# First loads, zero products, an early sine and norm, and turned blocks between products, in one decoder layer

## The chip, the cores and the metric

The kernel runs on one core of a Trainium2 chip. The metric is device time of one execution in microseconds. Three runs of the kernel before gave 999.52, 999.82 and 1001.32, so the median is 999.82.

## The reference, cut to what matters

One layer works on x of 256 tokens and 2048 channels, all in float32.

```python
h = rmsnorm(x, pre_mix_norm)
z = h @ w_in                       # 2048 -> 2048 conv (GLU) | 768 q latent | 512 kv latent | 64 rotary key
a, g = split(conv_in); u = a * sigmoid(g)
u = causal_depthwise_conv(u, conv_w, conv_b)            # 31 taps, 1024 channels
u = silu(layernorm(u))
q = rmsnorm(q_lat) @ w_uq ; kv = rmsnorm(kv_lat) @ w_ukv   # 8 heads, rotary parts with cos, sin
attn = causal_attention(q, k, v)
x = x + rmsnorm(concat(rmsnorm(u), rmsnorm(attn)) @ w_out)
x = x + rmsnorm(SwiGLU(rmsnorm(x)))                        # 2048 -> 5632 -> 2048
```

The scale of the first norm (one number per token) is not applied to h: the products with `w_in` are made from x times the gain, and the scale is applied to their results. So the products can start before the norm of x is known.

## The kernel before, in words

Weights come from memory as float32. Each is split into two float16 parts: ScalarE writes the high part (`whi`, line 108) and VectorE the rest (`wlo`, line 109). A product of two such numbers is three products on TensorE: high by high (line 153), high by low (line 154) and low by high (line 155), in `mm3`. A block of 128 input channels (one k) with two blocks of 128 tokens is thus six products of 512 columns.

`Weights.load` (line 124) brings a weight in pieces. One DMA fills a tile of `stage`, of which there are four, and one split fills a tile each of `whi` and `wlo`, of which there are eight. An ordinary piece is 1 MB, four k of 512 columns. The first weight, `wg0`, comes in pieces of 1, 1, 2, 2, 2, 4 and 4 k (line 211), each in a tile of its own, and `load_x` brings the same k of the transposed x ahead of each and splits them (lines 181 to 184). A piece can be fetched only when its stage tile has been read by both splits. All these loads stand in the DMA queue of SyncE (SP), one behind the other.

The second weight, `wg1`, follows. Its third piece has the two halves of x itself ahead of it in the queue (`load_tokens`, line 214). Behind `wg1` come four small loads: the rotary frequencies, the positions, the taps and the vectors of the convolution (lines 221 to 227). From the first two, VectorE makes the angles (lines 231 to 250) and ScalarE their sines (line 251). From x itself ScalarE makes four sums of squares (line 259), from which `r_half` and `r_x` follow by VectorE and GpSimd (POOL).

Then there is a loop over four groups of 512 columns (line 303): `mm3`, then for each block of tokens a tanh (line 312), a scaled copy (line 314), a product on VectorE (line 316), two transposes on TensorE (line 319) and a copy into `upad` (line 320). Behind each group `pump` issues some taps of the convolution: 3, 8, 13 and 14 (line 36). A tap is two multiply-adds on VectorE (line 289), or two products on ScalarE (line 295) and one addition on VectorE (line 297). Taps depend on `upad` and the taps before, and fill VectorE between other work. Three groups of 448 columns follow for the latents and the rotary key (line 357), with 11, 16 and 9 taps behind them. The norms of the latents are made in `latent_norm` (line 339), whose results are transposed by DMAs in the SP queue (line 346), and the rotary key is turned, with a transpose on TensorE (lines 371 to 386). Queries, values, attention, the output product and the feed-forward part follow.

The order of instructions on each engine is drawn at compile time, by a scheduler that takes the earliest written instruction that is ready by its own estimate of times. What is written later can so be put ahead of what its estimate has as not ready. On the chip each engine keeps that order. `add_manual_dep` with `NO_SYNC` adds an order, without a wait between engines.

Of the kernel before, what the change touches and what calls it, by code (L numbers as in the profile page):

```python
# [10 lines left out]
F16 = mybir.dt.float16  # L11
# [6 lines left out]
P = 128  # L18
# [17 lines left out]
PUMPS = dict(conv=(3, 8, 13, 14), lat=(11, 16, 9), v=(1, 0), uqp=3, head=(2, 7, 4, 8, 4, 4, 9, 8))  # L36
NG = 22
# [23 lines left out]
def hymba_layer(ctx: ExitStack, tc: tile.TileContext, x, xT, pos, inv_freq, g_pre, w_in, w_lat,  # L61
# [45 lines left out]
    def split(hi, lo, src, scale):  # L107
        nc.scalar.activation(hi, src, AF.Copy, scale=scale)  # L108
        nc.vector.scalar_tensor_tensor(lo, src, scale, hi, op0=ALU.mult, op1=ALU.subtract)  # L109
# [6 lines left out]
    class Weights:  # L116
# [7 lines left out]
        def load(self, src, scale, first=None, before=None):  # L124

            n = self.n
            per = self.kpb
            k0 = 0
            pieces = list(first or [])
            while k0 < self.kt:  # L130
                kk = pieces.pop(0) if pieces else per
                kk = min(kk, self.kt - k0)
                st = stage.tile([P, 2048], F32, tag="stage", name=nm("st"))
                if before is not None:
                    before(k0, k0 + kk)
                nc.sync.dma_start(st[:, : kk * n], src[:, k0 * n : (k0 + kk) * n])
                for j in range(0, kk, self.kpb):
                    w = min(self.kpb, kk - j) * n
                    hi = wsp.tile([P, 2048], F16, tag="whi", name=nm("whi"))
                    lo = wsp.tile([P, 2048], F16, tag="wlo", name=nm("wlo"))  # L140
                    split(hi[:, :w], lo[:, :w], st[:, j * n : j * n + w], scale)
                    for i in range(min(self.kpb, kk - j)):
                        self.parts.append((hi[:, i * n : (i + 1) * n], lo[:, i * n : (i + 1) * n]))
                k0 += kk
            return self

    def mm3(ps, x_of, wgt, tbs=(0, 1), k0=0, start=True, stop=True):
# [26 lines left out]
    nc.scalar.dma_start(gpre, g_pre)  # L174
    nc.vector.tensor_scalar(gpre, gpre, X_S, None, op0=ALU.mult)
# [35 lines left out]
    wg0 = Weights(KD, 512).load(w_in[0], W_S, first=[1, 1, 2, 2, 2, 4, 4], before=load_x)  # L211
    h_of = flat(hpool_h, hpool_l)

    def load_tokens(k0, k1):
# [5 lines left out]
    ifreq = const.tile([P, HALF], F32, name="ifreq")  # L220
    nc.sync.dma_start(ifreq, inv_freq)
    pos_i = const.tile([P, NTB], I32, name="pos_i")
    nc.sync.dma_start(pos_i, pos)
    cw = region(26.5, (CB, TAPS))
    nc.sync.dma_start(cw, conv_w)
    cv = const.tile([P, 4, CB], F32, name="cv")
    nc.sync.dma_start(cv, conv_v)
# [3 lines left out]
    nc.vector.tensor_copy(pos_f, pos_i)  # L231
# [25 lines left out]
    for tb in range(NTB):  # L257
        for i in range(2):
            nc.scalar.activation(junk_tile(1024), x_sb[:, tb, i * 1024 : (i + 1) * 1024], AF.Square,
                                 accum_out=ss_x[:, 2 * tb + i : 2 * tb + i + 1])  # L260
# [42 lines left out]
    for j in range(4):  # L303
        if j == 0:
            ps = ps0
        else:
            wgt = wg1 if j == 1 else Weights(KD, 512).load(w_in[j], W_S)
            ps = [acc_tile(), acc_tile()]
            mm3(ps, h_of, wgt)
        for tb in range(NTB):  # L310
            th = work.tile([P, 256], F32, tag="A", name=nm("th"), bufs=3)
            nc.scalar.activation(th, ps[tb][:, 256:512], AF.Tanh, scale=r_half[:, tb : tb + 1])
# [4 lines left out]
            tp = tmp_tile()  # L317
            for i in range(2):
                nc.tensor.transpose(tp[:, i * P : (i + 1) * P], u[:, i * P : (i + 1) * P], ident)
            nc.scalar.copy(upad[:, 2 * j : 2 * j + 2, PAD + tb * P : PAD + (tb + 1) * P],  # L320
                           tp[:, : 2 * P].rearrange("p (c t) -> p c t", c=2))
        conv_todo += [(j, k) for k in range(TAPS)]
        pump(PUMPS["conv"][j])

# [32 lines left out]
    for j in range(3):  # L357
        wgt = Weights(KD, LN).load(w_lat[j], W_S)
        ps = [acc_tile()[:, :LN], acc_tile()[:, :LN]]
        mm3(ps, h_of, wgt)  # L360
# [627 lines left out]
```

## Time and profile before

| what | us |
|---|---|
| median of three runs | 999.82 |
| time of the profiled execution | 1001.55 |
| its span in the trace | 999.70 |
| TensorE busy in the span | 959.6 |
| VectorE busy | 876.3 |
| ScalarE busy | 578.1 |

The 1.85 us between the profiled time and its span lie around the traced work. The span is the sum of the time in which TensorE works and the time in which it waits, so a stage is read by what TensorE waits for in it, and by the clock at which it works. Most of the kernel lies behind the stages that the change touches: these end at about 180 us.

### The profile page before, as it was taken

What the parts mean: (1) busy time and instruction counts of PE and PEld (TensorE: products, weight loads), DVE (VectorE), ACT (ScalarE), POOL (GpSimd) and SP (SyncE); (2) the same over time, 40 slices, a digit from 0 to 9 for tenths busy, and PEclk for the clock granted to TensorE, in tenths of its full rate; (3) what the DMA queues carried; (4) which work ended last, traced back from release to release, by engine and by line L of the source; (5) the groups of instructions that cost most, each with busy time, mean ns of one, the idle gap of its engine ahead of it and who ended that gap; (6) DMA issues with size and microseconds to landing.
All of it is one profiled execution on the core that took longest, in us unless ns stands there. A gap on an engine that the chain in (4) does not pass through costs nothing.

```text
span 999.7 us, 11980 instructions
## 1 busy us (share of the span) xinstructions
PE 959.6 (96%) x4577; PEld 454.4 (45%) x4577; DVE 876.3 (88%) x1024; ACT 578.1 (58%) x632; POOL 33.6 (3%) x50
## 2 busy tenths in 40 slices
PE   6999997999899998999999999999999999999995
PEld 2444553775444443444444444444444444444442
DVE  6799999999967999989898997897996988899855
ACT  7796764664666555655656645654663565555521
POOL 0000000033100100000000000000000000000000
PEclk9999998999999999999999999999999999999998
DMA  8974656476654966776875874784686646645532
GB/s 340 346 262 126 243 197 192 154 247 211 211 210 118 325 167 197 256 278 197 320 214 178 317 236 155 272 288 156 220 309 234 218 185 246 238 175 220 210 127 85
DMA packets 84010, 221.95 MB, mean 222 GB/s; under 512 B 55792, under 2 KB 56432, under 8 KB 61424
## 3 DMA queue, kind: packets, MB, share of 16 engines
q1 hardware_dynamic: 83232, 220.26, 63.7%
q10 hardware_dynamic: 720, 0.93, 0.3%
q8 instruction: 36, 0.59, 0.2%
q14 instruction: 22, 0.18, 0.1%
HBM read 204.25 MB, written 4.19 MB: 209 GB/s over the span
## 4 chain that ended last, share of the span: by engine, by line
PE 60%; DVE 23%; issue 5%; ACT 4%; DMA 3%; POOL 1%; SPq 0%; DVEq 0%; POOLq 0%; ACTq 0%
PE acc L740 10%; PE acc L741 10%; PE acc L739 10%; PE tmp L741 6%; PE tmp L740 6%; PE tmp L739 6%; DVE wlo L695 6%; DVE arena L289 3%; DVE wlo L109 3%; DVE st L709 2%; PE acc L155 2%; PE acc L153 2%; PE acc L154 2%; DMA st<-in_w_gu 2%; POOL sm L207 1%
## 5 line engine op out<-in xcount | busy, mean ns | idle before, releaser
L694 ACT ACTIVATE whi<-st 128x2048 f16<-128x2048 f32 (+1 forms) x177 | 317.1, 1798 | 228.7 <-PE acc L741 77.6
L695 DVE SCALAR_TENSOR_TENSOR wlo<-st,whi 128x2048 f16<-128x2048 f32 (+1 forms) x177 | 375.2, 2150 | 52.9 <-ACT whi L694 52.5
L740 PE MATMUL acc<-wlo,arena 128*128 128x512 f16 x620 | 235.0, 379 | 4.7 <-DVE wlo L695 4.7
L739 PE MATMUL acc<-whi,arena 128*128 128x512 f16 x620 | 235.0, 379 | 2.5 <-DVE q L773 1.4
L741 PE MATMUL acc<-whi,arena 128*128 128x512 f16 x620 | 235.0, 379 | 0.0
L153 PE MATMUL acc<-whi,arena 128*128 128x512 f16 (+1 forms) x380 | 143.5, 378 | 5.5 <-ACT whi L108 5.5
L741 PEld LDWEIGHTS <-arena 128*128 128x128 f16 x951 | 93.0, 98 | 117.4 <-issue 5.6
L154 PE MATMUL acc<-wlo,arena 128*128 128x512 f16 (+1 forms) x380 | 143.4, 377 | 2.2 <-DVE wlo L109 2.0
L740 PEld LDWEIGHTS <-arena 128*128 128x128 f16 x951 | 93.0, 98 | 114.3 <-issue 2.4
L739 PEld LDWEIGHTS <-arena 128*128 128x128 f16 x951 | 93.0, 98 | 113.3 <-DVE a L796 1.2
L155 PE MATMUL acc<-whi,arena 128*128 128x512 f16 (+1 forms) x380 | 143.3, 378 | 0.0
L739 PE MATMUL tmp<-whi,arena 128*128 128x512 f16 x331 | 125.4, 379 | 0.0
L740 PE MATMUL tmp<-wlo,arena 128*128 128x512 f16 x331 | 125.4, 379 | 0.0
L741 PE MATMUL tmp<-whi,arena 128*128 128x512 f16 x331 | 125.4, 379 | 0.0
L109 DVE SCALAR_TENSOR_TENSOR wlo<-st,whi 128x2048 f16<-128x2048 f32 (+4 forms) x59 | 118.2, 2009 | 6.5 <-ACT whi L108 6.5
L709 DVE TENSOR_TENSOR st<-st 128x1024 f32<-128x1024 f32 x135 | 117.2, 868 | 4.1
L108 ACT ACTIVATE whi<-st 128x2048 f16<-128x2048 f32 (+4 forms) x59 | 98.5, 1677 | 34.4 <-PE acc L155 10.3
L289 DVE SCALAR_TENSOR_TENSOR arena<-arena 128x256 f32<-128x256 f32 x184 | 78.5, 488 | 0.0
L153 PEld LDWEIGHTS <-arena 128*128 128x128 f16 x380 | 37.8, 99 | 47.4 <-ACT arena L113 5.0
L155 PEld LDWEIGHTS <-arena 128*128 128x128 f16 x380 | 37.8, 99 | 44.8 <-issue 5.1
L154 PEld LDWEIGHTS <-arena 128*128 128x128 f16 x380 | 37.6, 99 | 42.3 <-issue 2.8
L295 ACT ACTIVATE x_sb<-arena 128x256 f32<-128x256 f32 x56 | 25.3, 506 | 10.1 <-DVE arena L297 10.1
(209 smaller groups left out, 667.9 us busy)
## 6 DMA issues: line engine op xcount, KB each, us to landing
st<-in_w_gu SPq DMA_DIRECT2D x88, 1024.0 KB, 5.5
st<-in_w_dn SPq DMA_DIRECT2D x44, 1024.0 KB, 5.0
st<-in_w_out SPq DMA_DIRECT2D x16, 1024.0 KB, 5.1
st<-in_w_in SPq DMA_DIRECT2D x14, 1024.0 KB, 9.2
st<-in_w_lat SPq DMA_DIRECT2D x12, 896.0 KB, 5.5
x_sb<-in_x SPq DMA_DIRECT2D x4, 1024.0 KB, 8.6
st<-in_w_uqn SPq DMA_DIRECT2D x4, 768.0 KB, 4.9
st<-in_w_uv SPq DMA_DIRECT2D x2, 1024.0 KB, 5.9
```

Source lines behind the costliest of these rows:

```text
L108: nc.scalar.activation(hi, src, AF.Copy, scale=scale)
L109: nc.vector.scalar_tensor_tensor(lo, src, scale, hi, op0=ALU.mult, op1=ALU.subtract)
L153: nc.tensor.matmul(p_ap, xh, wh, start=(start and k == 0), stop=False)
L154: nc.tensor.matmul(p_ap, xh, wl, start=False, stop=False)
L155: nc.tensor.matmul(p_ap, xl, wh, start=False, stop=(stop and k == wgt.kt - 1))
L289: nc.vector.scalar_tensor_tensor(cacc[:, cb, :], upad[:, cb, k : k + S], cw[:, cb, k : k + 1], cacc[:, cb, :], op0=ALU.mult, op1=ALU.add)
L694: self.chain("ACT", nc.scalar.activation(hi[:, :n], src, AF.Copy, scale=scale))
L695: self.chain("DVE", nc.vector.scalar_tensor_tensor(lo[:, :n], src, scale, hi[:, :n], op0=ALU.mult, op1=ALU.subtract))
L709: self.chain("DVE", nc.vector.tensor_tensor(d, p, m, op=ALU.add))
L739: nc.tensor.matmul(ps, ah, bh, start=key not in self.begun, stop=False)
L740: nc.tensor.matmul(ps, ah, bl, start=False, stop=False)
L741: nc.tensor.matmul(ps, al, bh, start=False, stop=last)
```

## The change

- The pieces of `wg0` keep their sizes, but pieces 1, 1, 2 share one tile of `stage`, `whi` and `wlo`, and so do pieces 2, 2. The whole weight takes four tiles of each kind.
- A tile of zeros is set by VectorE, one sine of one column of it is made on ScalarE, and seven products of 512 columns of these zeros stand first on TensorE. Their result is not read.
- Frequencies and positions are loaded from ScalarE's queue at the start. The two halves of x, the taps and the vectors are loaded ahead of the second piece of `wg1` rather than the third.
- Three orders are added: the cast of the positions stands behind the last split of `wg0` on VectorE, the squares of the second half of x behind the first high part of `wg1` on ScalarE, and the first tanh behind its second high part.
- The work behind a group is parted in two. `glu` makes tanh, copy and product at once. `turn` holds the transposes, the copy into `upad` and the taps, and is called inside the next group's `mm3`: ahead of its k = 6 in group 1, of its k = 3 in groups 2 and 3 and in the first latent group. So it is also written behind the load of the next weight and no longer ahead of it.

The short description of the change also names a rotary key ahead of taps and sums over channel blocks by pairs. The diff, whose core follows, has no line on either.

```diff
+WARM = 7
+    def behind(ins, other):
+        tc.add_manual_dep(ins.ins, other.ins.name, NO_SYNC, reason="order")
...
-        def load(self, src, scale, first=None, before=None):
+        def load(self, src, scale, pieces=(), before=None):
+            for k0 in range(0, self.kt, self.kpb):
+                kb = min(self.kpb, self.kt - k0)
                 st = stage.tile([P, 2048], F32, tag="stage", name=nm("st"))
+                hi = wsp.tile([P, 2048], F16, tag="whi", name=nm("whi"))
+                lo = wsp.tile([P, 2048], F16, tag="wlo", name=nm("wlo"))
+                j = 0
+                while j < kb:
+                    kk = pieces.pop(0) if pieces else kb
+                    c = slice(j * n, (j + kk) * n)
+                    if before is not None:
+                        before(k0 + j, k0 + j + kk)
+                    nc.sync.dma_start(st[:, c], src[:, (k0 + j) * n : (k0 + j + kk) * n])
+                    h, self.last = split(hi[:, c], lo[:, c], st[:, c], scale)
+                    self.his.append(h)
+                    j += kk
...
+    def mm3(ps, x_of, wgt, tbs=(0, 1), k0=0, start=True, stop=True, at=()):
         for k in range(wgt.kt):
+            if k in at:
+                at[k]()
...
+    zeros = region(20, (512,), F16)
+    nc.vector.memset(zeros, 0.0)
+    nc.scalar.activation(zeros[:, 0:1], zeros[:, 0:1], AF.Sin)
+    warm = tmp_tile()
+    for i in range(WARM):
+        nc.tensor.matmul(warm, zeros[:, 0:P], zeros, start=True, stop=True)
+    ifreq = const.tile([P, HALF], F32, name="ifreq")
+    nc.scalar.dma_start(ifreq, inv_freq)
+    pos_i = const.tile([P, NTB], I32, name="pos_i")
+    nc.scalar.dma_start(pos_i, pos)
...
-    wg0 = Weights(KD, 512).load(w_in[0], W_S, first=[1, 1, 2, 2, 2, 4, 4], before=load_x)
+    wg0 = Weights(KD, 512).load(w_in[0], W_S, pieces=(1, 1, 2, 2, 2), before=load_x)
...
-        if k0 == 8:
+        if k0 == 4:
             for tb in range(NTB):
                 nc.sync.dma_start(x_sb[:, tb, :], x[:, tb, :])
+            nc.sync.dma_start(cw, conv_w)
+            nc.sync.dma_start(cv, conv_v)
...
-    nc.vector.tensor_copy(pos_f, pos_i)
+    behind(nc.vector.tensor_copy(pos_f, pos_i), wg0.last)
...
+            if tb == 1:
+                behind(sq, wg1.his[0])
...
+    def glu(j, ps):
+        us = []
         for tb in range(NTB):
...
+            if j == 0:
+                behind(t, wg1.his[1])
...
+            us.append(u)
+        def turn():
+            for tb, u in enumerate(us):
+                tp = tmp_tile()
+                for i in range(2):
+                    nc.tensor.transpose(tp[:, i * P : (i + 1) * P], u[:, i * P : (i + 1) * P], ident)
+                nc.scalar.copy(upad[:, 2 * j : 2 * j + 2, PAD + tb * P : PAD + (tb + 1) * P],
+                               tp[:, : 2 * P].rearrange("p (c t) -> p c t", c=2))
+            conv_todo.extend((j, k) for k in range(TAPS))
+            pump(PUMPS["conv"][j])
+        return turn
+    turn = glu(0, ps0)
+    for j in range(1, 4):
+        wgt = wg1 if j == 1 else Weights(KD, 512).load(w_in[j], W_S)
+        ps = [acc_tile(), acc_tile()]
+        mm3(ps, h_of, wgt, at={6 if j == 1 else 3: turn})
+        turn = glu(j, ps)
...
-        mm3(ps, h_of, wgt)
+        mm3(ps, h_of, wgt, at={3: turn} if j == 0 else ())
```

## Rows read from the trace of the kernel before

**Rows 1.** The page, busy time of each engine (share of the span) and instructions.

```profile
PE 959.6 (96%) x4577; PEld 454.4 (45%) x4577; DVE 876.3 (88%) x1024; ACT 578.1 (58%) x632; POOL 33.6 (3%) x50
```

**Rows 2.** Waits from 0 to 300: total us, times, longest us.

```profile
PE tmp L385 <- DVE kp L384: 6.2, 1, 6.2
...
PE tmp L319 <- DVE u L316: 2.4, 3, 1.0
```

**Rows 3.** Windows of 20 us: length, busy by engine, clock, DMA.

```profile
40.00:60.00 20.00, 19.47 (x94) 9.17 (x93) 18.50 (x39) 18.03 (x27) 0.00 (x0) 1.00 0.69 242
...
100.00:120.00 20.00, 20.00 (x108) 10.45 (x108) 20.00 (x31) 13.27 (x15) 0.00 (x0) 1.00 0.87 303
```

**Rows 4.** Timeline of TensorE, start: start, length, instruction, idle before and releaser.

```profile
5.51 0.59 PE L153 MATMUL acc<-whi,arena 128*128 128x512 f16 x1 [5.51 <-ACT whi L108]
...
10.88 0.63 PE L153 MATMUL acc<-whi,arena 128*128 128x512 f16 x1
12.12 0.38 PE L154 MATMUL acc<-wlo,arena 128*128 128x512 f16 x1 [0.61 <-DVE wlo L109]
12.34 0.38 PE L155 MATMUL acc<-whi,arena 128*128 128x512 f16 x1
...
21.68 0.38 PE L154 MATMUL acc<-wlo,arena 128*128 128x512 f16 x1 [1.41 <-DVE wlo L109]
```

**Rows 5.** Timeline of ScalarE, 0 to 56 us.

```profile
3.13 1.28 ACT L113 ACT_TABLE_LOAD   x1 [3.13 <-DMA arena<-in_xT]
4.43 0.51 ACT L113 ACTIVATE arena<-arena,gpre 128x256 f16<-128x256 f32 x1
...
17.39 1.91 ACT L108 ACTIVATE whi<-st 128x2048 f16<-128x2048 f32 x1 [0.78 <-DMA st<-in_w_in]
...
26.19 1.91 ACT L108 ACTIVATE whi<-st 128x2048 f16<-128x2048 f32 x1 [0.65 <-DMA st<-in_w_in]
...
31.78 1.06 ACT L259 ACTIVATE junk<-x_sb 128x1024 bf16<-128x1024 f32 x1 [0.84 <-DMA x_sb<-in_x]
...
35.73 0.47 ACT L312 ACTIVATE th<-acc,r_half 128x256 f32<-128x256 f32 x1 [1.62 <-DVE row_u L594]
...
44.58 1.28 ACT L251 ACT_TABLE_LOAD   x1
...
53.18 1.28 ACT L312 ACT_TABLE_LOAD   x1
```

**Rows 6.** Timeline of VectorE: a split, the cast of the positions, the first taps.

```profile
19.33 2.29 DVE L109 SCALAR_TENSOR_TENSOR wlo<-st,whi 128x2048 f16<-128x2048 f32 x1 [1.80 <-ACT whi L108]
...
40.25 0.16 DVE L231 CAST pos_f<-pos_i 128x2 f32<-128x2 int32 x1
...
48.31 2.46 DVE L289 SCALAR_TENSOR_TENSOR arena<-arena 128x256 f32<-128x256 f32 x6
```

**Rows 7.** Timeline of the SP queue: two late issues of first pieces.

```profile
6.21 0.35 SPq L136 DMA_DIRECT2D st<-in_w_in  x1
...
12.10 4.21 SPq L136 DMA_DIRECT2D st<-in_w_in  x3
```

**Rows 8.** Windows of 1 us, columns as in Rows 3: DMA early and full.

```profile
5.00:6.00 1.00, 0.49 (x1) 0.19 (x2) 0.96 (x2) 0.85 (x2) 0.00 (x0) 1.00 0.62 160
...
14.00:15.00 1.00, 1.00 (x7) 0.47 (x5) 1.00 (x3) 0.79 (x2) 0.00 (x0) 1.00 1.01 426
```

**Rows 9.** Timeline of ScalarE at the end of the latent groups.

```profile
154.35 1.06 ACT L108 ACTIVATE whi<-st 128x1024 f16<-128x1024 f32 x1 [3.96 <-DMA st<-in_w_uk]
157.28 1.48 ACT L108 ACTIVATE whi<-st 128x1536 f16<-128x1536 f32 x1 [1.88 <-DMA st<-in_w_uqn]
158.67 0.62 ACT L362 ACTIVATE arena<-acc,r_x 128x448 f32<-128x448 f32 x1
```

**Rows 10.** Timeline of TensorE there.

```profile
162.63 0.48 PE L385 MATMUL tmp<-ident,kp 128*128 128x128 f32 x1 [6.24 <-DVE kp L384]
...
168.62 0.38 PE L153 MATMUL acc<-whi,arena 128*128 128x512 f16 x1
```

More of the change, by code (lines that the diff above doesn't have):

```diff
@@ L107, in split @@
     def split(hi, lo, src, scale):
-        nc.scalar.activation(hi, src, AF.Copy, scale=scale)
-        nc.vector.scalar_tensor_tensor(lo, src, scale, hi, op0=ALU.mult, op1=ALU.subtract)
+        h = nc.scalar.activation(hi, src, AF.Copy, scale=scale)
+        return h, nc.vector.scalar_tensor_tensor(lo, src, scale, hi, op0=ALU.mult, op1=ALU.subtract)
+    def behind(ins, other):
+        tc.add_manual_dep(ins.ins, other.ins.name, NO_SYNC, reason="order")
     def split_g(hi, lo, src, g):
@@ L122, in __init__ @@
             self.parts = []
-        def load(self, src, scale, first=None, before=None):
+        def load(self, src, scale, pieces=(), before=None):
             n = self.n
[L127 to L132, printed above, removed]
-                st = stage.tile([P, 2048], F32, tag="stage", name=nm("st"))
[L134 to L144, printed above, removed]
+            pieces = list(pieces)
+            self.his = []
+            for k0 in range(0, self.kt, self.kpb):
+                kb = min(self.kpb, self.kt - k0)
+                st = stage.tile([P, 2048], F32, tag="stage", name=nm("st"))
+                hi = wsp.tile([P, 2048], F16, tag="whi", name=nm("whi"))
[10 more added lines that the diff above has]
+                    j += kk
+                for i in range(kb):
+                    self.parts.append((hi[:, i * n : (i + 1) * n], lo[:, i * n : (i + 1) * n]))
@@ L145, in load @@
             return self
-    def mm3(ps, x_of, wgt, tbs=(0, 1), k0=0, start=True, stop=True):
+    def mm3(ps, x_of, wgt, tbs=(0, 1), k0=0, start=True, stop=True, at=()):
         for k in range(wgt.kt):
+            if k in at:
+                at[k]()
             wh, wl = wgt.parts[k]
@@ L208, in rstd_of @@
         return r
-    wg0 = Weights(KD, 512).load(w_in[0], W_S, first=[1, 1, 2, 2, 2, 4, 4], before=load_x)
+    wg0 = Weights(KD, 512).load(w_in[0], W_S, pieces=(1, 1, 2, 2, 2), before=load_x)
     h_of = flat(hpool_h, hpool_l)
+    cw = region(26.5, (CB, TAPS))
+    cv = const.tile([P, 4, CB], F32, name="cv")
     def load_tokens(k0, k1):
-        if k0 == 8:
+        if k0 == 4:
             for tb in range(NTB):
                 nc.sync.dma_start(x_sb[:, tb, :], x[:, tb, :])
+            nc.sync.dma_start(cw, conv_w)
+            nc.sync.dma_start(cv, conv_v)
     wg1 = Weights(KD, 512).load(w_in[1], W_S, before=load_tokens)
[L220 to L227, printed above, removed]
     ps0 = [acc_tile(), acc_tile()]
@@ L258, in hymba_layer @@
         for i in range(2):
-            nc.scalar.activation(junk_tile(1024), x_sb[:, tb, i * 1024 : (i + 1) * 1024], AF.Square,
-                                 accum_out=ss_x[:, 2 * tb + i : 2 * tb + i + 1])
+            sq = nc.scalar.activation(junk_tile(1024), x_sb[:, tb, i * 1024 : (i + 1) * 1024], AF.Square,
+                                      accum_out=ss_x[:, 2 * tb + i : 2 * tb + i + 1])
+            if tb == 1:
+                behind(sq, wg1.his[0])
     ss_t = smalls(2)
@@ L301, in pump @@
             conv_tap(*conv_todo.pop(0))
[L303 to L308, printed above, removed]
-            mm3(ps, h_of, wgt)
+    def glu(j, ps):
+        us = []
         for tb in range(NTB):
             th = work.tile([P, 256], F32, tag="A", name=nm("th"), bufs=3)
-            nc.scalar.activation(th, ps[tb][:, 256:512], AF.Tanh, scale=r_half[:, tb : tb + 1])
+            t = nc.scalar.activation(th, ps[tb][:, 256:512], AF.Tanh, scale=r_half[:, tb : tb + 1])
+            if j == 0:
+                behind(t, wg1.his[1])
             av = work.tile([P, 256], F32, tag="B", name=nm("av"), bufs=3)
@@ L316, in hymba_layer @@
             nc.vector.scalar_tensor_tensor(u, th, 1.0, av, op0=ALU.add, op1=ALU.mult)
[L317 to L323, printed above, removed]
+            us.append(u)
[15 more added lines that the diff above has]
+        turn = glu(j, ps)
     z_all = region(16, (NTB, KL + QL + ROPE))
```

1 line of the change is left out of this document (removed).

## The prediction

> **What bounds the kernel now.** I read the page first: TensorE is busy for 959.6 of 999.7 us [rows 1], so it waits for only 40 us, and a change saves what it takes from these waits or from the time at half clock. Then I asked the view of waits for the stages that the diff touches: up to 300 us TensorE has one wait of 6.2 us before the transpose of the rotary key, three before the transposes of the conv groups, 2.4 us together [rows 2], and two for low parts of the first weight, 0.61 and 1.41 us [rows 4]. The windows say why so little else: TensorE works all the time and VectorE nearly does, 18.50 us of 20 from 40 to 60 and 20.00 from 100 to 120, yet between 22 and 153 us no product waits for a split [rows 2, 3]. TensorE is the bound there, and VectorE is full because taps fill it. So whatever brings TensorE forward before 153 us goes through, as long as splits stay ahead.
>
> The timelines of the start give the order there. TensorE waits 5.51 us for its first product, works at half clock for 13 products (0.63 us each, 5.37 us from the first to the thirteenth, so 0.45 us apart) and at full clock from 12.12 on (0.38 us each, the next start 0.215 behind, 512 columns at 2.4 GHz and a little) [rows 4]. At 21.68 it has waited 1.41 us for the low part of the sixth piece (k = 8 to 11). That low part is made from 19.33 to 21.62 [rows 6], behind a high part of 17.39 to 19.30 that waited for its DMA [rows 5]. So the path to 21.68 is landing, 1.91 us on ScalarE, 2.29 us on VectorE. From there TensorE does not wait before 55 us.
>
> **Part 1, pieces that share tiles.** Seven pieces in seven stage tiles, of which there are four, make SP wait: the fifth piece is issued at 6.21 and the last at 12.10 [rows 7]. Meanwhile the DMA engines are not full: 160 GB/s from 5 to 6 us, where the full rate is 426 [rows 8]. With four tiles for the whole weight nothing is waited for, and the queue is full from its first byte to the end of `wg0`. What that is worth: the gap lies between 4 and 7 us. If the small pieces run at about 340 GB/s at best, some 0.15 MB are won in each of these three us, 0.45 MB in all, 1.1 us at 426 GB/s. If they could run at 426, it is 0.27 MB each, 0.8 MB, 1.9 us, and a little more behind 7 us. The lower bound is 0, should the small loads that now run beside them cost as much as is won. I take 1.4 us, near the first, since small pieces are what runs there: the sixth piece lands at 16.0, its low part is ready at 20.2, and the products behind it run 1.4 us earlier.
>
> TensorE must by then be through with k = 0 to 7. These are 48 products: from about 5.8 us on, with all 13 slow ones kept, 13 x 0.45 + 35 x 0.215 = 13.4 us, the end at 19.2. That is before 20.2, so this part holds without any help from the zero products.
>
> **Part 2, zero products and the sine first.** The zeros are ready when VectorE has set them, the table for the sine is loaded (1.28 us, as at 44.58) and one column is done, an estimate of 2.7 us. Seven products 0.45 us apart last to 5.8, about where the first real one starts now. The table load of 3.13 no longer stands between the first x and its split [rows 5]: ScalarE starts 1.3 us earlier, less up to 0.4 us for issuing two small loads. So the first real product is ready earlier but waits for the zeros: nothing won or lost there, between -0.5 and 0.5 us. What the zeros could give is full clock earlier: at most 13 x (0.45 - 0.215) = 3.0 us of slow products. I take 0 of it for the sum, because the low part at 20.2 ends last either way. It would pay only if landing gained more than 2.4 us.
>
> The clock needs work, and it lasts over the wait of 1.41 us: the product at 21.68 takes 0.38 us, as before it [rows 4]. After 6.24 us without products it is down [rows 10]. The Trainium skill (TensorE: Matmul & The Clock Gate, Part 1: The HAM clock gate) has it that slow is the default and sustained activity releases it, with the moment set by a window that runs freely. By that rule the zeros buy full clock some 3 us sooner, and since the moment varies this also makes the start vary; the sum by it is the same, by the paragraph above.
>
> For the table, Sin is now followed by copies without a load, as behind 44.58, and the next load stands before the first tanh. One of three loads goes (3.13, 44.58, 53.18) [rows 5]; the one at 53.18, in the path of the transposes of group 1, is paid in the shadow of group 1's products. The Trainium skill (ScalarE: Activation LUTs, What ACT_TABLE_LOAD costs) adds a drain of about 1.4 us to each switch. The trace disagrees: the load starts at 3.13 and the split behind it at 4.43, so 1.3 us is all. By the page a load less would be worth 2.7 us of ScalarE.
>
> **Part 3, x ahead of the second piece of `wg1`.** Two halves of x (2.1 MB) and small loads come ahead of that piece, which lands 5.2 us later at 426 GB/s, less 1.4: its high part starts at 26.19 + 3.8 = 30.0 instead of 26.19 [rows 5], the low part is ready at 34.2. TensorE comes to it 24 products into group 1. `wg0` ends at 21.7 + 46 x 0.215 = 31.6 now, 30.2 then; plus 5.2 gives 35.4. The margin is 1.2 us, and no wait is added; with a landing 3 us later it would be 1.8 us. In return x lands one piece of 2.5 us earlier, plus 1.4: at 27.9 instead of 31.78. `r_half` follows some 4 us earlier, and the first tanh at about 32 to 33 instead of 35.73, behind the second high part and its table load. The rotary angles, on VectorE from 40.25 on, go to its idle time behind `wg0`. So the first taps start about 6 to 8 us before 48.31 [rows 6]. VectorE has that lead; TensorE doesn't wait for it, so I count 0, with up to 1 us where splits come earlier.
>
> **Part 4, transposes inside the next products.** They stood as soon as the scheduler thought their inputs ready, and TensorE waited three times, 2.4 us in all [rows 2]. Behind k = 2 of the next group there are 18 products, 3.9 us (3.4 in the latent group), between a group's end and its transposes. What has to be done in it, by an estimate, is four operations on ScalarE of the tanh's 0.47 us [rows 5] and a last product on VectorE of about a sixth of 2.46 us [rows 6], 2.3 us, so the cover is enough by 1 us or more if ScalarE is free, and not if a high part of 1.91 us stands ahead. I take 2.2 of the 2.4 us, bounds 0.5 and 2.4. Taps and `upad` are written behind the next weight's splits now; they are fill, and cost nothing as long as VectorE has others to do.
>
> **The sum.** 1.4 + 0 + 0 + 2.2 = 3.6 us up to 153 us. Behind it comes the wait of 6.24 us for the rotary key [rows 10]. Its chain goes over ScalarE, which holds the copy of the latents (line 362) to 158.67 behind two high parts that waited 3.96 and 1.88 us for DMAs [rows 9]. Those loads hang on stage tiles that VectorE frees and on the SP queue. With VectorE ahead of where it was, I give 0.4 us for it, bounds -6 and 8.7 (below). That makes 4.0 us: 1001.55 - 4.0 = 997.55 for an execution like the profiled one, and 995.8 from the median, which lies 1.73 below the profiled time. All behind 180 us shifts with TensorE, since no wait there is for something of fixed time.
>
> **The rivals.**
> A, the sum, 994 to 997.8.
> B, the wait for the rotary key goes as well. If the two high parts no longer stand waiting ahead of line 362, up to 3.96 + 1.88 = 5.84 us go, and with it the half clock behind the wait (from 162.63 to 168.62 [rows 10], some 14 products, 2.9 us). All of it is 8.7 us: 987.1. Half of it is likelier, 991. For it: VectorE's lead, and loads that wait for its splits. Against: the order there is drawn from estimates that the change doesn't touch. That the kernel also has the rotary key ahead of taps, which the diff lacks, would end here too.
> C, the start is won and given back: TensorE reaches the rotary key 3.6 us earlier but the loads and transposing DMAs of the SP queue keep their times, so the wait grows from 6.24 to about 10. Then nothing is won: 998 to 1001.8, at the middle 999.8. For it: SP and ScalarE wait there for DMAs, not for TensorE. Against: SP's loads are released by splits, which also come earlier.
> D, slower: in the newly drawn order one more whole weight piece stands ahead of line 362 on ScalarE. Its price is a landing of 1 MB (2.5 us) and both splits (1.91 + 2.29), 6.7 us on the wait, from which the 4.0 are taken: 999.8 + 2.7 = 1002.5. It decides if that piece's DMA is issued later than 3 us before the last latent product. For it: the loads for the next weights are now written ahead of the taps, so splits move forward on both engines. Against: two are already ahead.
>
> **How the numbers follow.** A 0.50, B 0.24, C 0.15, D 0.11. A change under 0.2% (2.0 us) can't be told from none here. Faster holds nearly all of A and B, 0.73; same C and a little of A, 0.16; slower D, 0.11. The range reaches from 989.0, leaving out the far end of B (0.06), to 1000.0, leaving out the end of C and all of D (0.14).
>
> **What would show it.** SP issues all pieces of `wg0` without a gap, DMA at over 300 GB/s from 4 to 7 us, and the product that now waits at 21.68 starts near 20.3: part 1. Seven products before the first of line 153 and no table load at line 113: part 2. No wait of TensorE at k = 4 of group 1: part 3. No waits of line 319's transposes: part 4. The wait for `kp` at 6 us, 3.6 us earlier: A. It is wrong if TensorE's products at the end of the latent groups come less than 2 us earlier, or if the wait for `kp` changes by over 3 us.

## The result and the profile after

The change makes the kernel slower. Five runs of it gave a median of 1005.88 us (1005.20 to 1007.49), beside five of the kernel before with 999.82 (999.30 to 1002.10). The ratio is 1.0057, with a 95% interval of 1.0041 to 1.0072. The forecast was 995.8 us, so its sign was wrong. The profiled execution took 1005.29 us, with a span of 1003.5.

The page first, busy time of each engine, which answers to [rows 1].

```profile
PE 964.4 (96%) x4584; PEld 457.1 (46%) x4584; DVE 876.1 (87%) x1025; ACT 578.5 (58%) x632; POOL 34.9 (3%) x50
```

TensorE is busy for 4.8 us longer. Of these, 2.96 us are the seven products of zeros (3.21 to 6.17 us), and they stand where it waited before. Behind its first real product it works for 1.8 us longer than before and waits for 1.3 us longer, so the loss is partly waiting and partly work at the lower clock. The waits of TensorE from 0 to 300 us, as in [rows 2] (total us, times, longest):

```profile
PE tmp L416 <- DVE kp L415: 6.8, 1, 6.8
PE tmp L191 <- ACT arena L188: 3.2, 1, 3.2
PE tmp L518 <- POOL ss L512: 2.6, 2, 2.3
PE acc L164 <- DVE wlo L110: 2.4, 2, 1.7
PE tmp L517 <- POOL ss L512: 2.3, 1, 2.3
```

The wait of the conv groups' transposes is gone, as intended. The wait for the rotary key stayed (line 416 is line 385 of before). And two waits have grown from 1.0 to 4.9 us together, in attention, a stage that the diff does not touch: transposes of scaled scores that wait for GpSimd. In before they were:

```profile
PE tmp L486 <- POOL ss L481: 0.7, 1, 0.7
PE tmp L487 <- POOL ss L481: 0.3, 1, 0.3
```

Windows of three stages, of before, of after, and of the ninth experiment below (`e9`), with the columns of [rows 3]: length, busy time (and count) of PE, PEld, DVE, ACT, POOL, granted clock, DMA share, GB/s. Before:

```profile
80.00:153.00 73.00, 72.15 (x371) 36.20 (x370) 72.12 (x116) 44.11 (x59) 1.64 (x2) 1.00 0.57 188
153.00:180.00 27.00, 20.76 (x88) 9.50 (x87) 24.54 (x55) 16.02 (x25) 1.17 (x2) 0.87 0.56 178
180.00:215.00 35.00, 34.03 (x249) 26.61 (x246) 33.42 (x76) 23.83 (x50) 6.70 (x9) 1.00 0.56 186
```

After:

```profile
80.00:153.00 73.00, 72.24 (x373) 36.30 (x372) 72.13 (x119) 42.84 (x59) 1.43 (x2) 1.00 0.56 178
153.00:180.00 27.00, 20.24 (x90) 9.15 (x89) 24.85 (x59) 15.77 (x27) 1.18 (x2) 0.87 0.72 191
180.00:215.00 35.00, 30.32 (x198) 23.27 (x197) 27.55 (x61) 18.76 (x37) 9.53 (x8) 0.90 0.53 185
```

The changed kernel in another order (`e9`):

```profile
153.00:180.00 27.00, 22.39 (x125) 12.06 (x124) 26.14 (x61) 17.75 (x31) 1.17 (x2) 1.00 0.76 212
180.00:215.00 35.00, 33.68 (x233) 25.81 (x232) 32.98 (x76) 24.23 (x50) 8.62 (x12) 1.00 0.54 183
```

Read the counts of PE and the clock together. In the same 35 us of attention the changed kernel gets 198 products done instead of 249, and 0.90 is the mean of a clock that was at half (1.2 GHz) in two stretches, 198.2 to 201.6 and 208.5 to 211.9. From 153 to 180 us both kernels run at half clock for 6.8 us around the wait for the key; the last kernel has none there.

The table below follows the same products through all traces: the start of each minus its start in the trace of before, in us. "End of latents" is the third product behind the last latent one; "key" is the first transpose of the rotary key; "scores" are the first and the fifteenth instruction of line 461 (492 in after), the products of queries and keys.

```
                               ninth  end of                scores   scores  first feed-
                               k      latents   key         1        15      forward   end
before, start                  21.89  153.63    162.63      188.34   208.66  326.50    949.22
after                          -0.74   -2.09     +0.87       -1.43    +5.51   +5.05    +3.83
e1 after, old order attention  -0.44   -1.64     +1.32       -0.12    -0.12   +0.78    -0.52
e2 before, new order attention -0.08   +0.72     -1.00      -1.08   +10.56  +10.08   +10.09
e3 no zeros, order of after    -0.21   -1.40     +1.56      -0.14   +7.72   +7.29    +6.33
e4 transposes alone, held      -0.20   -1.86     -1.17       -0.90    -0.89   -1.16    -1.41
e5 e1, key first               -0.55   -1.74     -5.70       +3.49    +3.50   +3.24    +3.48
e6 e1, no zeros                -0.64   -1.83     +1.13       -0.84    -0.84   -1.11    -2.16
e7 front alone, attention held -0.20   +1.80     +0.05       +4.81    +4.81   +4.83    +3.83
e8 after, two splits later     -0.78   -1.98     +0.97       -1.50    -1.49   +1.64    +0.06
e9 after, old order latents    -0.82   -1.88     -5.31       -5.92    -5.92   -5.90    -7.83
e10 e5, splits behind key      -0.11   -1.29     -4.95       -1.08    -1.08   -1.06    -1.31
e11 e5, transposes first on SP -0.03   -1.22     -5.17       +0.07    +0.07   -0.21    -0.93
e12 front alone, latents held  -0.85   +1.00     -0.69       -0.98    -0.98   -1.23    -2.16
```

So the change wins 2.1 us by the end of the latents, loses them at the key, gets some back (21 products of the rotary query stand ahead of its key, 14 in before), and loses 6.9 us between the two marks of the scores. Differences of half a microsecond say little: e1, e5, e10 and e11 have one order up to 154 us, and their ninth k spreads from -0.55 to -0.03. The last column says little either: in before, products of the feed-forward part waited 1.8 us in two places where e9 did not wait.

### The profile page after: what moved, and what is told of

It reads as the page before. It is cut to its first block, busy times and chain, and to the rows that moved or that the text cites. A ratio compares the mean times of both kernels' runs of the same rounds, so it can differ in the third digit from the quotient of the medians.

```text
span 1003.5 us, 12002 instructions
## 1 busy us (share of the span) xinstructions
PE 964.4 (96%) x4584; PEld 457.1 (46%) x4584; DVE 876.1 (87%) x1025; ACT 578.5 (58%) x632; POOL 34.9 (3%) x50
## 4 chain that ended last, share of the span: by engine, by line
PE 54%; DVE 27%; issue 9%; DMA 4%; ACT 3%; POOL 2%; DVEq 0%; SPq 0%; POOLq 0%; ACTq 0%
PE acc L770 10%; PE acc L771 10%; PE acc L772 10%; PE tmp L770 6%; PE tmp L771 6%; PE tmp L772 6%; DVE wlo L726 6%; DVE wlo L110 5%; DVE arena L309 5%; DMA st<-in_w_gu 2%; DVE st L740 2%; DMA st<-in_w_in 2%; DVE arena L317 1%; PE acc L165 1%; PE acc L163 1%
```

## The experiments

Four sets of kernels ran, each beside runs of the kernel before: 1000.31 us in the set of e1 to e4, 1000.63 (e5 to e8), 1000.93 (e9 to e11) and 1001.43 (e12 by itself). So ratios are compared across sets, not times.

Since the scheduler draws the order of each engine again when anything is changed, most kernels hold an order. The kernel records a place in its list of instructions, and at its end adds, for each engine, an order without waits between all that was written since:

```diff
+    def keep_order():
+        want = json.loads(zlib.decompress(base64.b85decode(ORDER)))
+        made = list(nc.cur_bb.bb.instructions)[mark[0]:]
+        for name, ranks in want.items():
+            mine = [i for i in made if str(i.engine).split(".")[-1] == name]
+            for a, b in zip(ranks, ranks[1:]):
+                tc.add_manual_dep(mine[b], mine[a].name, NO_SYNC, reason="order")
```

From the first projection of attention on, the instructions of both kernels are the same ones. Their order is not: TensorE's differs in 254 of 3738 places, VectorE's in 129 of 753, ScalarE's in 61 of 439, GpSimd's in 6 of 33.

**e1, the changed kernel with the order of before from attention on.** The edit is the block above, with the mark at the first head's projection and `ORDER` taken from the kernel before.

> The changed kernel whole, but from the first projection of attention to the end each engine's instructions are held in the order that they had in the kernel before. Theory (the loss lies in the order that was drawn anew from attention on): TensorE keeps the 1.4 us that it was ahead at the first scores, has no half clock between 195 and 215 us, and the time falls by 5 to 8 us from 1005.9, to 998 to 1001. Rival (VectorE, ScalarE or the loads arrive at attention later than before, whatever the order): the time stays at 1004 to 1007.

999.89 us, ratio 0.9992 (0.9983 to 1.0002). The loss is gone: TensorE is at -0.12 us at both marks of the scores, though not at the 1.4 us ahead that I expected it to keep. The order of attention alone costs the changed kernel about 6.5 us (1.0057 against 0.9992), and the change without it costs nothing.

**e2, the kernel before with the order of after from attention on.** The same block in the kernel before.

> The kernel before, unchanged up to attention, but from the first projection on each engine's instructions are held in the order of the changed kernel. Theory (the order alone costs it): slower than before by 5 to 8 us, 1005 to 1008, with waits for the scaled probabilities and half clock between 195 and 215 us. Rival (the state in which the engines arrive): 999 to 1001, as before.

1010.37 us, ratio 1.0095 (1.0080 to 1.0110). Without one line of the diff, the new order makes the old kernel 10 us slower, more than the 5 to 8 expected, and where it does so is the same place: +11.6 us between the two marks of the scores. So the cause lies in the order. Its price is not the same in the two kernels (6.5 and 10 us), and why was not tried. Ahead of attention e2 isn't quite before: 12 products stand ahead of its key instead of 14.

**e3, no zero products, order of after.** It leaves out products whose result nothing reads.

```diff
-    warm = tmp_tile()
-    for i in range(WARM):
-        nc.tensor.matmul(warm, zeros[:, 0:P], zeros, start=True, stop=True)
```

> The changed kernel without its seven zero products, the rest of it the same, and from attention on the order of the changed kernel held. Theory (the zeros let TensorE come to the sixth piece early, wait longer and fall to half clock at 20.7 us): no half clock between 20 and 24 us, first-group products 1.5 to 2.5 us earlier than in the changed kernel, 1003 to 1004.5 in all. Rival (the wait for the sixth piece brings half clock with or without zeros, or TensorE without zeros is itself late by as much): 1005 to 1007.

1007.91 us, ratio 1.0072 (1.0060 to 1.0084). I had blamed the zeros for a stretch at half clock from 20.7 to 24.1 us in the profiled execution of after, in which TensorE lost 1.5 us. That theory fell: without zeros the stretch was missing, but so it was in e1, which has them, and the time did not fall; it even came out above the rival's range. What e3 has is a longer stretch at half clock in attention (196.7 to 203.5). It stays open why.

**e4, only the transposes moved, order of before from attention on.** The front of the kernel before, with `glu`, `turn` and `at` of the change.

> The kernel before with the one part that calls the transposes inside the next group's products, and from attention on the order of the kernel before held. Theory (the three waits of 2.4 us go and nothing else changes): TensorE is 2.0 to 2.4 us earlier at the end of the latent groups, and the time is 997 to 998.5 if the wait for the rotary key stays at 6.2 us. Rival (the wait for the rotary key takes it back): the wait grows by about 2 us, 999.5 to 1000.5.

998.84 us, ratio 0.9986 (0.9977 to 0.9994). That is a little above the 997 to 998.5 expected. Part 4 by itself is worth 1.66 us at the end of the latents (-1.86, of which -0.20 stood at the ninth k already): 0.8 of the 2.4 us of waits stayed.

**e5, e1 with the rotary key ahead on VectorE.** In the trace of after the copies of the latents are early, and the key is still late. VectorE shows why (start, length, instruction):

```profile
152.56 1.76 DVE L110 SCALAR_TENSOR_TENSOR wlo<-st,whi 128x1536 f16<-128x1536 f32 x1
154.22 2.46 DVE L309 SCALAR_TENSOR_TENSOR arena<-arena 128x256 f32<-128x256 f32 x6
156.60 2.89 DVE L110 SCALAR_TENSOR_TENSOR wlo<-st,whi 128x1024 f16<-128x1024 f32 x2
...
159.47 0.18 DVE L409 TENSOR_TENSOR kt<-arena,sincos 128x32 f32<-128x32 f32 x1
...
163.25 0.19 DVE L415 COPY kp<-kp 128x64 f32<-128x64 f32 x1
```

And ScalarE, the copies that the key reads (line 393 is line 362 of before):

```profile
154.79 1.14 ACT L393 ACTIVATE arena<-acc,r_x 128x448 f32<-128x448 f32 x2
```

Against 158.67 in [rows 9] the copy is 3.9 us earlier. But six taps and two splits, 5.3 us of work, were drawn ahead of the key, and VectorE keeps that order. The edit, on VectorE's order alone:

```diff
-6 taps, 2 splits, key (14) with norm (6), a split and an addition between
+key (14), norm (6) with 3 taps between, 3 taps, 2 splits, split, addition
```

> The changed kernel with the kernel before's order from attention on (999.89 us as run), its whole instruction order held, and on VectorE alone the rotary key (14 instructions) and the kv norm (6) moved ahead of the six taps and two splits that stand between the latents and them. Nothing else moves. My theory: the transposes of the rotary key wait because VectorE takes 5.3 us of taps and splits first (six taps from 154.69 for 2.46 us, two splits from 157.06 for 2.88), not because of SP or of a DMA. Then the copy of the key ends near 157 to 158 instead of 163.71, the wait is about 1 to 2 us instead of some 8, the half clock behind it (159.6 to 169.9) goes or is shorter, and the time is 992 to 996. Rival: the transposing DMAs or the first weights' loads end last there, as case C of the prediction had it; then the wait moves to the products behind the key and the time is 998 or more. Second rival: the taps, now later, hold up the splits of the next weights; then TensorE waits for a split at the query latents and the time is 996 to 999.

1005.57 us, ratio 1.0041 (1.0026 to 1.0055). Half of the theory held: the key's transposes started at 156.93 without a wait. Then the first rival struck, harder than expected. TensorE and the SP queue of e5:

```profile
172.44 0.61 PE L324 MATMUL acc<-whi,arena 128*128 128x512 f16 x1 [11.89 <-DMA arena<-arena]
```

```profile
164.10 0.33 SPq L307 DMA_DIRECT2D st<-in_w_uk  x1
165.77 0.33 SPq L307 DMA_DIRECT2D st<-in_w_uqn  x1
166.15 5.05 SPq L538 DMA_TRANSPOSE arena<-arena  x2
```

The norm of the kv latents was done by 161.7, but the DMAs that transpose its results stood behind two loads, and these waited for stage tiles that the two splits free, which I had moved back.

**e6, e1 without zero products.**

> The changed kernel without the zero products, with the kernel before's order from attention on, as in the first run of this order (999.89 us with zeros). It tells what the zeros are worth where the order cannot be redrawn. By the first trace with zeros full clock is reached some 4.5 us earlier than before; if the sixth piece ends last either way the zeros are worth nothing, 999.5 to 1000.3. If the slow products cost what they take (13 at 0.45 instead of 0.215 us) they are worth up to 3 us: 1002 to 1003. If they only move the moment at which the clock falls later, either sign up to 1.5 us.

1000.03 us, ratio 0.9990 (0.9981 to 1.0000). Against 0.9992 with zeros there is no difference.

**e7, the front alone, order of before from attention on.** Pieces, zeros, sine and norm as in the change, the loop of the kernel before.

> Only the front of the change (pieces of shared tiles, zero products, sine and norm of x early), the loop over the conv groups as in the kernel before, the order from attention on that of the kernel before. My theory by landmarks: the front brings TensorE 0.4 to 0.8 us forward at the seventeenth k-step, which the turn alone (998.84) doesn't have; with the waits of the conv groups' transposes left in, 1 us at most is won before the rotary key, and the time is 998.5 to 1000.5. Rival: the front's earlier loads are what puts taps and splits ahead of the rotary key, and the wait there grows here too: 1000.5 to 1003. If the front is free of that, the wait for the key stays at 6 us or below and the time is below 999.5.

1006.65 us, ratio 1.0050 (1.0038 to 1.0062): the rival, and worse. The six taps and two splits stand ahead of the key here too. Then the rotary query is late: two waits of 2.5 us together, and half clock from 177.3 to 180.7. So the front is what puts the taps ahead of the key.

**e8, the changed kernel with two splits on VectorE later.** In after, GpSimd's scaling of scores (line 512) takes far longer than in before. GpSimd and VectorE:

```profile
193.75 3.18 POOL L512 TENSOR_SCALAR ss<-ss,sm 128x128 f32<-128x128 f32 x2 [31.81 <-DVE sm L508]
...
203.04 3.58 POOL L512 TENSOR_SCALAR ss<-ss,sm 128x128 f32<-128x128 f32 x2 [1.85 <-DVE sm L508]
```

```profile
193.94 2.30 DVE L110 SCALAR_TENSOR_TENSOR wlo<-st,whi 128x2048 f16<-128x2048 f32 x1
...
204.08 2.28 DVE L110 SCALAR_TENSOR_TENSOR wlo<-st,whi 128x2048 f16<-128x2048 f32 x1
```

Beside each pair runs a split. The pair at 193.75 ends 0.69 us behind the split's end. TensorE waits, and soon afterwards the clock is at half: a projection's product takes 0.42 us, and 0.27 once the clock is back.

```profile
196.53 0.33 PE L517 MATMUL tmp<-ident,ss 128*128 128x128 f32 x1 [2.29 <-POOL ss L512]
...
200.11 0.42 PE L172 MATMUL tmp<-arena,whi 128*128 128x256 f16 x1
...
201.84 0.27 PE L172 MATMUL tmp<-arena,whi 128*128 128x256 f16 x1
```

The edit moves each of these two splits behind the next instructions of VectorE:

```diff
-split (193.94), row max of scores, addition of a tap
+row max of scores, addition of a tap, split
```

> The changed kernel with its own order, except that the two VectorE splits which run beside GpSimd's scaling of scores at 193.9 and 204.1 us stand behind the next tap (8 VectorE positions differ). My theory: GpSimd's scaling takes 3.2 and 3.6 us beside such a split and 1.1 to 1.4 us alone, TensorE's transposes of the scaled scores wait 2.3 and 2.6 us for it, and the clock then falls to half for 3.4 us each time. Without the overlap both scalings take under 1.5 us, the waits and the two half-clock stretches (198.2 to 201.6, 208.5 to 211.9) go, and the time falls by 3.8 to 7.2 us to 999 to 1002. If the tap slows GpSimd in the same way, or the order of TensorE in attention itself is the cause: 1005 to 1007. If only the waits go and the clock still falls: 1002 to 1004.

1001.71 us, ratio 1.0010 (1.0002 to 1.0019). Eight changed places on one engine give back 4.7 us of the ratio. GpSimd in e8:

```profile
193.67 0.98 POOL L673 TENSOR_SCALAR ss<-ss,sm 128x128 f32<-128x128 f32 x2 [31.62 <-DVE sm L669]
...
199.80 1.46 POOL L673 TENSOR_SCALAR ss<-ss,sm 128x128 f32<-128x128 f32 x2 [1.85 <-DVE sm L669]
```

The two stretches at half clock are gone, and one new one stands at 211.6 to 215.0, behind a wait of 1.7 us. So the theory holds for these two places. The other 1.8 of the 6.5 us were not traced to a place. The Trainium skill (SBUF — State Buffer, Who interferes with whom) has it that a VectorE instruction with two inputs in SBUF shares a read path with GpSimd instructions that read SBUF, and that the one which issues second stands until the other has ended. A split has two such inputs (`st`, `whi`). The trace agrees that one stands: the first scaling of the first pair took 2.72 us where the second took 0.48, and ended 0.24 us behind the split's end at 196.24. It does not show the order of the two: in the records the scaling that stood starts 0.19 us before the split. A tap on VectorE has two such inputs as well, but takes 0.48 us.

In before one scaling meets a split too, GpSimd first, then VectorE. It took 2.26 of the pair's 2.72 us, but TensorE did not wait for it:

```profile
205.24 2.72 POOL L481 TENSOR_SCALAR ss<-ss,sm 128x128 f32<-128x128 f32 x2 [4.66 <-PE tmp L493]
```

```profile
204.99 2.27 DVE L109 SCALAR_TENSOR_TENSOR wlo<-st,whi 128x2048 f16<-128x2048 f32 x1
```

**e9, the whole change with the order of e4 from the first latent product on.** The same block, with the mark ahead of the latent groups.

```diff
     LN = (KL + QL + ROPE) // 3
+    mark = [len(nc.cur_bb.bb.instructions)]
```

> The whole change, with the order of every engine from the first latent product on (not only from attention on) taken from the kernel in which the transposes alone were moved (998.84 us). So the rotary key stands right behind the latents' copies on VectorE again, with the six taps and two splits behind it. My theory: what the early loads won at the start (0.4 to 0.8 us at the seventeenth k-step) is kept, the copy of the key is late by the high part on ScalarE as before, the wait for it is 5 to 6 us as before: 998.0 to 999.0, at or just under the run with the transposes alone. Rival: with this order VectorE and SP, which are ahead at the start, stand waiting for TensorE, and nothing of the start is kept: 999 to 1000. If the front costs something in itself that the order does not explain: over 1000.5.

995.62 us, ratio 0.9945 (0.9933 to 0.9958), better than expected and the best of all: it beats the kernel before by 0.55% and the change by 1.1%. VectorE and ScalarE in e9:

```profile
152.76 1.75 DVE L257 SCALAR_TENSOR_TENSOR wlo<-st,whi 128x1536 f16<-128x1536 f32 x1
154.43 0.18 DVE L557 TENSOR_TENSOR kt<-arena,sincos 128x32 f32<-128x32 f32 x1
...
157.08 0.18 DVE L563 COPY kp<-kp 128x64 f32<-128x64 f32 x1
```

```profile
151.98 1.48 ACT L256 ACTIVATE whi<-st 128x1536 f16<-128x1536 f32 x1 [3.04 <-DMA st<-in_w_uqn]
...
153.76 1.14 ACT L541 ACTIVATE arena<-acc,r_x 128x448 f32<-128x448 f32 x2
```

The high part that waited for its DMA until 157.28 in [rows 9] starts at 151.98, the copies at 153.76, and the key follows at once, with all but one of the six taps and both splits behind the copy at 157.08. The transpose waits 3.04 us instead of 6.24 [rows 10], and the clock does not fall at all between 9.2 and 985.4 us.

**e10, e5 with the two splits right behind the key.**

> As the run with the rotary key moved ahead on VectorE (1005.57 us), but the two splits for the next weights come right behind the key, ahead of the kv norm, and only the six taps are moved back. In that run TensorE had no wait for the key, but one of 11.9 us for the transposing DMAs of the kv latents, which stood on the SP queue behind two loads that waited up to 9.7 us for a stage tile which these splits free. My theory: with the splits early the loads are issued by 160, the transposing DMAs by 162 to 163, the wait of 11.9 us becomes 3 to 5, and the time is 996 to 999. Rival: the norm itself, now 2.9 us later, and the transposing DMAs' own time (up to 5 us on SP) keep the wait over 7 us: 1000 to 1003.

999.24 us, ratio 0.9980 (0.9972 to 0.9989), just above the theory's 996 to 999. The wait of 11.9 us became 4.7 at the longest, and half clock from 165.3 to 172.1 stayed.

**e11, e5 with the transposing DMAs ahead of the two loads on the SP queue.**

> As the run with the rotary key moved ahead (1005.57 us), and on the SP queue the two transposing DMAs of the kv latents moved ahead of the two weight loads that stood in front of them. It tells whether the 11.9 us are the queue (case C of the prediction) or the norm. If the queue: the transposing DMAs are issued right behind the norm's splits, near 159.6 and 161.7, the wait falls to 3 to 5 us, and the next wait is for the rotary query behind three splits on VectorE: 997 to 1000. If the norm or the DMAs themselves: the wait stays above 9 us and the time at 1003 to 1006. The two loads come later by some 2 us; if that starves the projections of the heads, the products near 190 us wait, 1001 to 1004.

999.81 us, ratio 0.9991 (0.9982 to 1.0000), as for the queue. SP in e11:

```profile
160.20 3.28 SPq L538 DMA_TRANSPOSE arena<-arena  x2
```

Issued 6 us earlier, they leave a wait of 2.3 us instead of 11.9, and the rotary query waits 2.4 us next. So the 11.9 us were the queue.

**e12, the front alone with the order of before from the first latent product on.**

> The front alone (pieces, zero products, sine and norm of x), the loop over the conv groups as before, and the order of every engine from the first latent product on that of the kernel before. It splits the 5.3 us of the whole change in held order (995.62 against 1000.93) into its parts: the transposes alone gave 1.5 us (998.84 against 1000.31 in their session). The front alone with the order held only from attention on was 1006.65 and TensorE stood 1.80 us later than before at the end of the latents. My theory: what puts the latents' copies 5 us earlier is the lead of VectorE and SP that the front gives, so the wait for the key falls from 6.2 to about 3 us here too, and the conv groups' transposes keep their waits, 2.4 us and more: 996.5 to 999. Rival: the lead needs the transposes moved as well; then the copies stand where they did before, the wait stays at 6 us or more, and the 1.8 us lost by the end of the latents show: 1000 to 1003.

999.89 us, ratio 0.9986 (0.9975 to 0.9996), between the two. TensorE was 1.0 us late at the end of the latents, the copies stood at 157.98, nearly where they were before, and the wait for the key was 4.6 us instead of 6.2. Front alone 0.14%, transposes alone 0.14%, both together 0.55%. The issues of the load of the first query weight (uqp) on SP tell what that sum leaves out. With the transposes alone (e4):

```profile
123.75 4.64 SPq L268 DMA_DIRECT2D st<-in_w_uqp  x2
```

With both (e9):

```profile
119.59 4.64 SPq L293 DMA_DIRECT2D st<-in_w_uqp  x2
```

It is 126.02 in before and 125.19 in e12. In the held orders only both parts together bring the weights' queue to the end of the latents 4 to 6 us ahead; the first piece of `w_uk`, say, is issued at 149.95 in before, 149.11 in e12, 148.10 in e4 and 143.95 in e9. The order has a share in this: e12 holds that of before and e9 that of e4, and the front in an order of its own (e7) issues uqp at 123.33. And the front alone makes the waits of the conv groups' transposes longer, which part 4 then takes away; in e12 they are four and 3.6 us, where before had three and 2.4:

```profile
PE tmp L487 <- DVE u L484: 3.6, 4, 1.7
```

The changed kernel has the lead of the queue as well, and its order spends it on other work:

```profile
119.39 4.64 SPq L146 DMA_DIRECT2D st<-in_w_uqp  x2
...
137.47 0.33 SPq L146 DMA_DIRECT2D st<-in_w_uk  x1
```

The first of the two splits at 156.60, ahead of the key, is for the piece issued at 137.47. e9 issues its first such piece at 143.95 and splits it at 161.97, behind the key. How much of the lead comes from these waits was not tried.

## Why the prediction was wrong

**The step that failed** is "All behind 180 us shifts with TensorE, since no wait there is for something of fixed time", with the argument against B that "the order there is drawn from estimates that the change doesn't touch". I took the order behind the change as fixed; only case D had it redrawn, and there on ScalarE at the latents. The scheduler drew it anew, and in attention this put splits beside GpSimd's scalings in places where TensorE waits for them: 6.5 us (e1), of which two splits explain 4.7 (e8). In before these waits were 1.0 us, and a list of waits does not show which of them another order would bring. Neither of my two alarms rang: TensorE came 2.09 us earlier at the end of the latents (the bound was 2), and the wait for the key went from 6.2 to 6.8 us (the bound was 3). Both watched the stage that I had thought about.

**Second step: "Taps and `upad` ... are fill, and cost nothing as long as VectorE has others to do."** Fill is free only behind what TensorE waits for. Ahead of the key it took 5.3 us of VectorE, and with the old order from the latents on, on all engines (e9 against e1), 0.47% came back.

**Part 1**, 1.4 us: the direction was right, the size too large. SP issues all of `wg0` by 8.30, and DMA runs at 307 GB/s from 4 to 7 us (183 before), as I had asked. But ScalarE starts the sixth high part at 16.48 instead of 17.39 [rows 5], 0.9 us earlier, and the ninth k comes 0.03 to 0.85 us earlier in the eleven traces that have the front, 0.74 in after. Start of TensorE in after:

```profile
3.21 3.17 PE L191 MATMUL tmp<-arena 128*128 128x512 f16 x7 [3.21 <-ACT arena L188]
6.17 1.05 PE L163 MATMUL acc<-whi,arena 128*128 128x512 f16 x2
...
20.77 0.58 PE L164 MATMUL acc<-wlo,arena 128*128 128x512 f16 x1 [1.73 <-DVE wlo L110]
```

The last row answers to 21.68 in [rows 4]: I had 20.3. The low part still ends last, as I argued.

**Part 2**, 0 us: right (e6). The first real product starts at 6.17 instead of 5.51 [rows 4], behind the zeros, slightly outside my bound of 0.5. Full clock came at 7.1 us instead of 11.5 (from 6.0 to 9.2 in all traces with zeros, at 8.2 and 9.0 with the front but without them), and it bought nothing. The table load was followed by its user at once, as I had read it:

```profile
1.65 1.28 ACT L188 ACT_TABLE_LOAD   x1 [1.65 <-PEq L1008]
2.94 0.20 ACT L188 ACTIVATE arena<-arena 128x1 f16<-128x1 f16 x1
...
35.51 0.47 ACT L328 ACTIVATE th<-acc,r_half 128x256 f32<-128x256 f32 x1
```

**Part 3**, 0 us: no wait in group 1, as said. The first tanh hardly moved (35.51, I had 32 to 33; 35.73 in [rows 5]), since it stands behind a high part and its own table load. The first taps on VectorE began at 43.32 instead of 48.31 [rows 6], 5.0 us earlier and so less than the 6 to 8 forecast. I gave this lead no value. It had two: in the order drawn anew it was spent on taps and splits ahead of the key, and in e9, with the transposes moved, the weights' queue that is 4 to 6 us ahead lets the key go early.

**Part 4**, 2.2 us: 1.7 us (e4). In e9 one group's transposes still wait, 1.3 us in two waits for line 316's product. The cover was enough for most of them, not for all.

**The rotary key**, 0.4 us with bounds of -6 and 8.7: 0.7 us lost in after, from -2.09 at the latents to -1.43 at the first scores (the wait grew from 6.24 to 6.76 us), and 4.0 to the good in e9 (-1.88 to -5.92), where half of case B happened: high part out of the way, wait halved, no half clock. Case B was priced at 991 then, and e9 came to a ratio that is 994.3 us beside a median of 999.82. Case C, the SP queue with its loads ahead of the transposing DMAs, was the next limit as soon as VectorE's order let the key through (e5, e11). Case D had the right sign and the wrong mechanism: nothing more stood on ScalarE, all of it stood on VectorE.

So the sum of the parts, 995.8, is close to what the change comes to in a held order, 994.3, but that is luck: the start and the transposes gave 1.9 us instead of 3.6, and the key 4.0 instead of 0.4. In the kernel as it was made, 11 us of redrawn order came on top.

## What to carry to other kernels

Where a scheduler draws the order, an edit has two prices: the edit's own, and that of the order drawn around it, which can fall in a stage far behind (here 0.55% to the good and 1.1% to the bad). Compare the order of each engine before and after, name what is now ahead of the instructions that the bounding engine waits for, and price the edit by a run with the order held. Filling work belongs behind the short chain that is waited for, and a long split with two inputs does not belong beside a GpSimd operation on that chain.

## What the runs showed of the hardware that was not expected

- GpSimd's scalings of scores (128x128 and 128x256) took 2.72 to 2.76 us where a VectorE split of 2.3 us began about 0.2 us behind their start, in after, e2 and e3 alike. The other fourteen in after took 0.37 to 0.84 us.
- The length of a wait alone did not tell whether the clock fell. For the key, a wait of 6.8 us was met by half clock from 160.7 to 167.5 (after) and one of 3.04 us by none (e9); in attention one of 2.29 us, up to 196.53, was followed by half clock from 198.2. Near 245 us six kernels in the old order (e1, e4, e5, e6, e11, e12) have one and the same wait of 2.0 us for a scaling beside a split; half clock followed in e1 alone, from 245.0 to 248.4.
- A stretch at half clock that one profiled execution shows (20.7 to 24.1 us in after) can be missing in kernels with the same start (e1, and e8, whose order differs from that of after in eight places, all behind 193 us). One trace does not show that an edit causes it.
